# Holding a background decode back at the stage boundaries of a hybrid decoder step, with ScalarE's reads of a bank first and the last tile scaled late

## The chip, the cores and the metric

The kernel runs on one core of one Trainium2 chip. Its time is the device time of one execution in microseconds (us), as the median of several runs; lower is better. TensorE (PE in the profile) multiplies matrices into banks of the accumulation memory, VectorE (DVE), ScalarE (ACT) and GpSimd (POOL) work elementwise, and SyncE (SP) issues most of the transfers (DMAs). Every engine runs its own queue in order and waits on semaphores for the others.

## The reference

One layer of a hybrid decoder step, for two groups that share the weights: a prompt of 1024 rows and 8 sample rows with 8192 past tokens each, in a paged cache.

```python
h = rmsnorm(x) @ w_in                      # q, k, v (8 heads x 64), forget logits, u, z
att = softmax(q k^T / 8 + c_q - c_k, causal) @ v      # c: cumulated log-forget
sgu = u * (tril(w_s) applied to chunks of 128 of rmsnorm(z) + b_s)
x = x + concat(rmsnorm(att), rmsnorm(sgu)) @ w_o
x = x + cross_attention(rmsnorm(x), 256 memory tokens, 4 heads x 256) @ w_co
h = rmsnorm(x) @ w_up                      # 1024 -> 2 x 2816
hc = conv_b + sum_i conv_w[i] * h shifted by 2 - i rows      # causal, depthwise
x = x + (silu(gate(hc)) * val(hc)) @ w_down
y = rmsnorm(x)
```

For the sample rows the attention runs over the cache (`cache_k`, `cache_v`, gathered by a page table), and the convolution over a stored state. All of it is float32. The kernel returns both outputs and the new keys, values, log-forget gates, memory keys and values and convolution states.

## The kernel before

**Products.** Each large product is made of three: both operands are split into a rounded high part and a rest, and `gemm3` (L244, L245, L246) sums high x high, high x rest and rest x high. `split` makes the parts: ScalarE copies the high part (L207, or L210 with a scale), VectorE subtracts for the rest (L208, L211). Weights come through SyncE's queue as 512 KB pieces (`wr`) and are split into `wh` and `wl`. I call these three lines' 5568 matmuls the main matmuls, and count positions on TensorE by them.

**The prompt line.** `prompt()` is a generator. It runs the input projection (stage p1), the attention of both halves of 512 rows (att0, att1), and then for each half: `merge`, an output projection (`out_proj` with `w_o`), the cross stage (mid0, mid1; `norm_T`, queries, scores, and `out_proj` with `w_co`), the gated MLP (`ffn0`, `ffn1`: `norm_T`, then groups of up products with the convolution, and down products), and `final`. Each `yield` gives a cost in units of its work.

`out_proj` works on four tiles of 128 rows, two column halves each. `residual` adds the product to the rows (L905) and takes the sum of squares of each half (L202). For a projection whose rows are normalised next, `prepare(i)` adds both halves' sums on VectorE (L910), takes mean and EPS on VectorE (L195) and the power -1/2 on POOL (L196), and ScalarE scales the tile (L921). The last tile's is queued under `high_priority`.

`norm_T` transposes the first three tiles together on TensorE (L954), splits the eight transposed blocks (L210, L211) and runs the first product on these 384 columns; then it transposes the fourth tile (L968), splits it, and runs the product's other 128 columns.

In the convolution ScalarE reads a bank (L1132), VectorE reads it twice (L1133, L1134), and ScalarE reads its last two columns for the state (L1135); then the bank is free.

**The background.** `sample()` is a second generator with the sample rows' work: 128 steps on the keys (`kstep`: an indirect load of 1 MB into one of four `kv` buffers by POOL, L1246, a product and a reduction on VectorE, L1252 and L1256), softmax, 128 steps on the values (a load, L1305, and four matmuls, L1311), and then the rest: projections, the cross attention over the stored memory (VectorE's L1475 and L1476 on `kv`), 22 up steps (a 1 MB load, L1550, and eight matmuls, L1554; every second one followed by a fold, L1569), 11 down steps (a 1 MB load, L1588, and four matmuls, L1593) and the last sum (L1606). A load goes out when one of the four buffers is free.

The loop that emits both lines adds up the prompt line's units and advances the background by one step for every `PACE` units of the stage:

```python
PACE = {'p1': 7.5, 'att0': 20.0, 'mid0': 8.0, 'ffn0': 9.0, 'att1': 15.0, 'mid1': 7.5, 'ffn1': 2.5, 'rest': 3.3}
...
        acc[0] += t
        while bgs and acc[0] >= PACE[phase[1] or phase[0]]:
            acc[0] -= PACE[phase[1] or phase[0]]
            if next(bgs[0], None) is None:
                bgs.pop()
```

What is emitted goes through a scheduler that simulates the engines and fixes each engine's queue at build time. So the order on an engine follows the emission only loosely: what counts is where the built program puts an instruction.

Of the kernel before, what the change touches and what calls it, by code (L numbers as in the profile page):

```python
# [18 lines left out]
P = 128  # L19
D = 1024  # L20
# [58 lines left out]
def build(nc, tc, ctx, a, phases=None):  # L79
# [81 lines left out]
    nc.vector.memset(mhalf, -0.5)  # L161
    warm = const.tile([P, 1], F32, tag="warm", name="warm")
# [144 lines left out]
    def p1(early):  # L307
# [119 lines left out]
        for tt in range(8):  # L427
            ps, ps2 = BK(), BK()
            mm_chunk(tt, ws, ps[:, 0:260], 0, 260)
            mm_chunk(tt, ws, ps2[:, 0:260], 260, 260)  # L430
            if tt == SD - 1:
                sps = [sample_copy(*sp) for sp in sps]
            if tt == SD:
                sp = sample_sum(*sps[0])
                nc.scalar.activation(us, sp, AF.Gelu_apprx_tanh, scale=rsk)
                sp = sample_sum(*sps[1])
                nc.vector.scalar_tensor_tensor(fs, sp, rsk, bfb[:8], op0=ALU.mult, op1=ALU.add)
            nc.vector.scalar_tensor_tensor(fl[:, tt, :], ps[:, 0:8], rstd[:, tt : tt + 1], bfb, op0=ALU.mult, op1=ALU.add)
            u = T2()
            nc.scalar.activation(u[:, 0:252], ps[:, 8:260], AF.Gelu_apprx_tanh, scale=rstd[:, tt : tt + 1])  # L440
            nc.scalar.activation(u[:, 252:512], ps2[:, 0:260], AF.Gelu_apprx_tanh, scale=rstd[:, tt : tt + 1])
            nc.scalar.dma_start(sgu_d[tt * P : (tt + 1) * P, :], u)
            yield 5.4
# [111 lines left out]
    def gating(hf):  # L555
# [44 lines left out]
        r = rstd_of(ssu, AW, 4, "r4")  # L600
        for pr_ in range(2):
# [50 lines left out]
    def attention(hf, late=None, at=3):  # L652
# [16 lines left out]
        def setup(hp, qn, kn, vn):  # L669
# [4 lines left out]
            for j in range(2):  # L674
# [5 lines left out]
                nc.vector.tensor_tensor(qq[64:128, 0, :], tr[rows, :], qq[0:64, 0, :].bitcast(F32), op=ALU.subtract)  # L680
# [9 lines left out]
                nc.gpsimd.dma_start(kb[j][64:68, :], ck_d[h, :, : nk * P])  # L690
            for kh in range(hf + 1):
# [5 lines left out]
                for j in range(2):  # L697
                    rows = slice(64 * j, 64 * j + 64)
                    nc.scalar.activation(ka[j][0:64, s], tr[rows, :], AF.Copy)
                    if KP & 1 << hf:  # L700
                        nc.gpsimd.tensor_copy(ka[j][64:128, s], ka[j][0:64, s].bitcast(F32))
                    else:
                        nc.scalar.activation(ka[j][64:128, s], tr[rows, :], AF.Copy)
                    nc.vector.tensor_tensor(kb[j][0:64, s], tr[rows, :], ka[j][0:64, s].bitcast(F32), op=ALU.subtract)
# [149 lines left out]
    def close(hf, att):  # L854
# [4 lines left out]
        r = rstd_of(ssa, AW, 4, "r4")  # L859
        for b2 in range(2):  # L860
# [4 lines left out]
            nc.sync.dma_start(an_d[t0 * P : (t0 + 2) * P, :].rearrange("(c p) d -> p c d", p=P), att[b2])  # L865

# [30 lines left out]

    def squares():
        return sm([P, 4, 2], "sqx", 2)
# [13 lines left out]
    def out_proj(w, mh, ml, xt, fetch=None, ys=None):  # L913

        sq = squares()

        def prepare(i):
            r = rows_rstd(sq, i, i + 1)
# [3 lines left out]
            ys.append(y)  # L922

        korder = (4, 5, 6, 7, 0, 1, 2, 3)
        for n in range(2):
# [5 lines left out]
            for i in range(4):  # L931
# [6 lines left out]
                if ys is not None and n == 1 and i > 0:  # L938
                    prepare(i - 1)
                residual(xt, sq, i, n, ps)  # L940
                yield 5.2
        if ys is not None:
            with tc.high_priority():
                prepare(3)
        return sq

    def norm_T(ys, g0, first):
# [3 lines left out]
        for kk in range(8):  # L951
# [8 lines left out]
            if kk % 2:  # L960
                yield 0.8
        first(hs, ls, slice(0, 384))
# [8 lines left out]
        first(hs, ls, slice(384, 512))  # L971
        return hs, ls
# [126 lines left out]
    def ffn(hf, xt, ys, late=None):  # L1099
# [18 lines left out]
        for gi, gn in enumerate(GROUPS):  # L1118
            gh, gl = [], []
            for f in range(f0, f0 + gn):  # L1120
                hc2 = []
                for part in range(2):
# [9 lines left out]
                    nc.scalar.activation(hc, pv, AF.Identity, bias=cb, scale=cw[2])  # L1132
                    nc.vector.scalar_tensor_tensor(hc[:, 1:], pv[:, :511], cw[1], hc[:, 1:], op0=ALU.mult, op1=ALU.add)  # L1133
                    nc.vector.scalar_tensor_tensor(hc[:, 2:], pv[:, :510], cw[0], hc[:, 2:], op0=ALU.mult, op1=ALU.add)  # L1134
                    nc.scalar.activation(hlast[hf][:, ft, :], pv[:, 510:512], AF.Copy)  # L1135
# [504 lines left out]
    def prompt():  # L1640
# [26 lines left out]
        close(0, att)  # L1667
# [3 lines left out]
        else:  # L1671
            att = yield from att1
        ends = []
        for hf in range(2):
# [27 lines left out]
    for t in prompt():  # L1702
# [7 lines left out]
        while bgs and acc[0] >= PACE[phase[1] or phase[0]]:  # L1710
# [96 lines left out]
```

## Time and profile before

| | before |
|---|---|
| median of 3 runs | 1917.92 us (1917.23 to 1918.78) |
| the profiled execution's own time | 1925.17 us |
| its span in the trace | 1923.4 us |
| mean granted TensorE clock | 0.976 |
| busy: PE, DVE, ACT, POOL | 94%, 73%, 40%, 23% |
| moved by DMA | 517.07 MB, mean 269 GB/s |

Times in the trace are counted from the start of its span. A row of the chain of waits gives the waiting engine, tile and line, what released it, and the sum, the number and the longest of these waits. A row in order of time gives start, duration, engine, line, operation, output from inputs, shapes and count, and in brackets how long the engine had been idle before and what released it. Equal instructions that follow each other stand in one row, and a matmul of float32 operands leaves two records. A row of a window gives the stretch, then for PE, PEld (weight loads), DVE, ACT and POOL the busy time and the count, and at the end the granted clock, the share of the DMA engines that was busy and the GB/s.

### The profile page before, as it was taken

The numbers are of one execution on the slowest core, as the hardware profiler recorded it, in microseconds if no ns is written. First come the engines' busy times: TensorE is split into PE (matmuls) and PEld (weight loads), VectorE is DVE, ScalarE is ACT, GpSimd is POOL, SyncE is SP. The second block draws the span as 40 slices with busy tenths as digits, with TensorE's granted clock in tenths as the row PEclk, the third lists the DMA queues.
The fourth block names the chain that finished last, engine by engine and source line by source line (L and its number), as shares of the span: only waits on it lengthen the run. The fifth ranks groups of instructions, "written<-read, shape, count | busy, mean of one in ns | idle before, by whom it ended". The sixth has DMA issues, their size and how long they took to land.

```text
span 1923.4 us, 24228 instructions
## 1 busy us (share of the span) xinstructions
PE 1817.3 (94%) x9255; PEld 1300.1 (68%) x9255; DVE 1407.5 (73%) x1679; ACT 763.6 (40%) x1419; POOL 446.1 (23%) x427
## 2 busy tenths in 40 slices
PE   8999989888898998999999999998989999899998
PEld 5987667555576666777777776765756667667765
DVE  4887567877678768889899899878785548754344
ACT  5332366576532534433334234326234333242232
POOL 1222241222022323222112315131332012101110
PEclk9999999999998998999999999999989999999999
DMA  8876887744587858678777889977698657667972
GB/s 325 290 266 222 296 328 262 249 145 164 183 328 295 310 208 296 254 262 328 271 271 268 321 299 354 357 293 281 248 342 339 221 206 261 223 244 241 321 280 101
DMA packets 156372, 517.07 MB, mean 269 GB/s; under 512 B 20168, under 2 KB 41928, under 8 KB 123488
## 3 DMA queue, kind: packets, MB, share of 16 engines
q0 software_dynamic: 56400, 339.04, 47.4%
q1 hardware_dynamic: 92944, 163.89, 24.4%
q10 hardware_dynamic: 6912, 12.59, 1.7%
q8 instruction: 73, 1.20, 0.2%
q14 instruction: 43, 0.35, 0.1%
HBM read 493.63 MB, written 21.84 MB: 268 GB/s over the span
## 4 chain that ended last, share of the span: by engine, by line
PE 63%; DVE 7%; issue 6%; DMA 3%; ACT 2%; POOL 1%; POOLq 0%; DVEq 0%; ACTq 0%
PE ba L244 11%; PE ba L246 10%; PE ba L245 10%; PE bb L245 5%; PE bb L244 5%; PE bb L246 5%; PE dv L1311 5%; DVE kv L1252 1%; DVE s L1256 1%; PE dv L1554 1%; DVE wl L208 1%; DMA kv<-cache_v,kidx 1%; DMA t<-o_mk 1%; PE bb L763 1%; PE ba L719 1%
## 5 line engine op out<-in xcount | busy, mean ns | idle before, releaser
L207 ACT ACTIVATE wh<-wr 128x1024 fp32r<-128x1024 f32 (+2 forms) x220 | 228.9, 1044 | 410.8 <-PE ba L245 125.1
L208 DVE TENSOR_TENSOR wl<-wr,wh 128x1024 fp32r<-128x1024 f32 (+2 forms) x220 | 261.8, 1202 | 169.0 <-PE ba L246 73.3
L1252 DVE TENSOR_TENSOR kv<-kv,d 128x2048 f32<-128x2048 f32 (+1 forms) x139 | 292.2, 2114 | 34.7 <-DMA kv<-cache_k,kidx 34.7
L1256 DVE TENSOR_REDUCE s<-kv 128x32 f32<-128x2048 f32 (+1 forms) x139 | 291.9, 2107 | 0.7
L1246 POOL DMA_INDIRECT kv<-cache_k,kidx x128 | 166.0, 1297 | 487.1 <-DVE s L1256 242.1
L1305 POOL DMA_INDIRECT kv<-cache_v,kidx x128 | 159.8, 1249 | 490.3 <-PE dv L1311 196.0
L244 PE MATMUL ba<-wh,u 128*128 128x512 f32 (+1 forms) x679 | 261.5, 388 | 7.6 <-ACT u L210 3.9
L245 PE MATMUL ba<-wl,u 128*128 128x512 f32 (+1 forms) x679 | 259.7, 383 | 0.0
L246 PE MATMUL ba<-wh,u 128*128 128x512 f32 (+1 forms) x679 | 256.9, 383 | 0.4 <-DVE u L208 0.4
L244 PE MATMUL ba<-u,wh 128*128 128x512 f32 (+2 forms) x552 | 218.9, 397 | 0.0
L245 PE MATMUL ba<-u,wh 128*128 128x512 f32 (+2 forms) x552 | 216.9, 394 | 0.0
L246 PE MATMUL ba<-u,wl 128*128 128x512 f32 (+2 forms) x552 | 216.6, 393 | 0.0
L244 PEld LDWEIGHTS ba<-wh,u 128*128 128x128 f32 x679 | 129.0, 190 | 43.3 <-issue 9.5
L245 PEld LDWEIGHTS ba<-wl,u 128*128 128x128 f32 x679 | 128.8, 190 | 30.5 <-issue 5.5
L246 PEld LDWEIGHTS ba<-wh,u 128*128 128x128 f32 x679 | 128.4, 189 | 29.7 <-issue 3.4
L244 PEld LDWEIGHTS ba<-u,wh 128*128 128x128 f32 x552 | 105.7, 192 | 42.4 <-issue 14.5
L1311 PE MATMUL dv<-kv,s 128*32 128x512 f32 x1024 | 133.1, 620 | 0.1
L245 PEld LDWEIGHTS ba<-u,wh 128*128 128x128 f32 x552 | 106.2, 192 | 29.3 <-issue 8.4
L246 PEld LDWEIGHTS ba<-u,wl 128*128 128x128 f32 x552 | 105.7, 192 | 28.8 <-issue 6.8
L244 PE MATMUL bb<-wh,u 128*128 128x512 f32 (+1 forms) x313 | 120.7, 386 | 4.1 <-ACT hlast L1135 4.1
L245 PE MATMUL bb<-u,wh 128*128 128x512 f32 (+2 forms) x312 | 123.8, 397 | 0.6 <-DVE u L211 0.6
L244 PE MATMUL bb<-u,wh 128*128 128x512 f32 (+2 forms) x312 | 123.3, 395 | 0.1
(403 smaller groups left out, 2940.2 us busy)
## 6 DMA issues: line engine op xcount, KB each, us to landing
wr<-w_up SPq DMA_DIRECT2D x88, 512.0 KB
kv<-w_up POOLq DMA_DIRECT2D x22, 1024.0 KB, 8.1
wr<-w_down SPq DMA_DIRECT2D x40, 512.0 KB
kv<-w_down POOLq DMA_DIRECT2D x11, 1024.0 KB, 6.4
wr<-w_in SPq DMA_DIRECT2D x16, 512.0 KB
wr<-w_o SPq DMA_DIRECT2D x16, 512.0 KB
wr<-w_cq SPq DMA_DIRECT2D x16, 512.0 KB
wr<-w_co SPq DMA_DIRECT2D x16, 512.0 KB
```

The costliest lines, as they stand in the source:

```text
L207: nc.scalar.activation(h, src, AF.Copy)
L208: nc.vector.tensor_tensor(l, src, h.bitcast(F32), op=ALU.subtract)
L244: mmul(out, sh, mh, start=(i == 0), stop=False)
L245: mmul(out, sh, ml, start=False, stop=False)
L246: mmul(out, sl, mh, start=False, stop=(i == n - 1))
L719: mmul(s, qab[j][:, 0, i * P : (i + 1) * P], ka[j][:, ch * n : ch * n + n], start=True, stop=False)
L763: mmul(po[64 * j : 64 * j + 64, q0:256], vn[:, kt, 64 * j : 64 * j + 64], pt[j][kt // 4][:, kt % 4, q0:256], start=(kt == 0), stop=(kt == ...
L1246: nc.gpsimd.indirect_dma_start(kv, None, a["cache_k"], off(kidx[:, b, ch : ch + 1]))
L1252: nc.vector.tensor_tensor(kvv[:, i : i + m, :], kvv[:, i : i + m, :], qb.unsqueeze(1).broadcast_to((P, m, 512)), op=ALU.mult)
L1256: nc.vector.tensor_reduce(s[:, ch * 4 + i : ch * 4 + i + m, :].rearrange("p k h -> p (k h)"), kvv[:, i : i + m, :].rearrange("p k (h d) -> ...
L1305: nc.gpsimd.indirect_dma_start(kv, None, a["cache_v"], off(kidx[:, b, ch : ch + 1]))
L1311: mmul(dv[32 * j : 32 * j + 32, :], s[:, ch * 4 : ch * 4 + 4, :].rearrange("p k h -> p (k h)"), kvv[:, j, :], start=(ch == 0), stop=(ch == ...
```

## The change

- **Hold.** A flag `held` is set with the last tile of an `out_proj` and cleared at the end of the next `norm_T`. While it is set the loop advances no background step. The loop also takes at most `int(t / PACE) + 1` steps after one unit of the prompt line.
- **The factor.** `prepare` is split. `factor(i)` sums on ScalarE (the first half's sum goes through an Identity with EPS as bias into `part`, the second through another with `part` as bias), and POOL takes the power; VectorE has no part in it. `scaled` multiplies on ScalarE. For the last tile `scaled` is kept as a partial call, which `norm_T` makes after the splits of the first three tiles.
- **ScalarE first.** In the convolution the read of the last two columns moves ahead of VectorE's two reads. In the attention's set-up ScalarE reads both halves of a bank before VectorE subtracts from them. In the input projection the gelu of a bank stands ahead of VectorE's read of it.
- **Small pieces.** `stats` makes its two factors with two powers on POOL instead of one, a copy and a product. `close` (sums of squares and scaling of the attention's output) becomes a generator, whose steps run beside the attention of half 1 and beside `merge` instead of at once. `gating` has one more `yield`.

```diff
@@ stats, input projection
-            r = rstd_of(ssx[:, c], D, 4, "r4")
-            nc.vector.tensor_copy(rstd[:, c], r)
-            nc.vector.tensor_scalar(rstd8[:, c], r, 0.125, None, op0=ALU.mult)
+            for dst, m in ((rstd8, 64.0), (rstd, 1.0)):
+                v = sm([P, 4], "xv", 2)
+                nc.vector.tensor_scalar(v, ssx[:, c], m / D, m * EPS, op0=ALU.mult, op1=ALU.add)
+                nc.gpsimd.tensor_tensor(dst[:, c], v, mhalf[:, :4], op=ALU.pow)
...
@@ attention set-up
-                nc.vector.tensor_tensor(qq[64:128, 0, :], tr[rows, :], qq[0:64, 0, :].bitcast(F32), op=ALU.subtract)
...
+            for j, qq in enumerate(qab):
+                rows = slice(64 * j, 64 * j + 64)
+                nc.vector.tensor_tensor(qq[64:128, 0, :], tr[rows, :], qq[0:64, 0, :].bitcast(F32), op=ALU.subtract)
...
@@ close
         for i in range(4):
             ssq_into(ssa[:, i : i + 1], att[i // 2][:, i % 2, :])
-        r = rstd_of(ssa, AW, 4, "r4")
+        yield
+        r = rstd_of(ssa, AW, 4, "ra")
+        yield
...
+    def beside(main, steps, at):
+        n = 0
+        while True:
+            try:
+                t = next(main)
+            except StopIteration as e:
+                return e.value
+            yield t
+            if n in at:
+                next(steps)
+            n += 1
...
@@ out_proj
-        def prepare(i):
-            r = rows_rstd(sq, i, i + 1)
+        part = sm([P, 4], "part", 2)
+
+        def factor(i):
+            r = sm([P, 1], f"fac{i}", 2)
+            nc.scalar.activation(r, sq[:, i, 1:2], AF.Identity, scale=1.0 / D, bias=part[:, i : i + 1])
+            nc.gpsimd.tensor_tensor(r, r, mhalf[:, 0:1], op=ALU.pow)
+            return r
+
+        def scaled(i, r):
             y = U([P, D])
             for c in (slice(0, 512), slice(512, D)) if i == 3 else (slice(0, D),):
                 nc.scalar.activation(y[:, c], xt[i][:, c], AF.Copy, scale=r)
-            ys.append(y)
+            return y
...
                 if ys is not None and n == 1 and i > 0:
-                    prepare(i - 1)
+                    ys.append(scaled(i - 1, factor(i - 1)))
                 residual(xt, sq, i, n, ps)
+                if ys is not None and n == 0:
+                    nc.scalar.activation(part[:, i : i + 1], sq[:, i, 0:1], AF.Identity, scale=1.0 / D, bias=epsb)
+
+                held[0] = n == 1 and i == 3
                 yield 5.2
         if ys is not None:
             with tc.high_priority():
-                prepare(3)
+                ys.append(partial(scaled, 3, factor(3)))
@@ norm_T
+        if callable(ys[3]):
+            ys[3] = ys[3]()
         first(hs, ls, slice(0, 384))
         yield 4
...
         first(hs, ls, slice(384, 512))
+        held[0] = False
@@ ffn, convolution
                     nc.scalar.activation(hc, pv, AF.Identity, bias=cb, scale=cw[2])
+                    nc.scalar.activation(hlast[hf][:, ft, :], pv[:, 510:512], AF.Copy)
                     nc.vector.scalar_tensor_tensor(hc[:, 1:], pv[:, :511], cw[1], hc[:, 1:], op0=ALU.mult, op1=ALU.add)
                     nc.vector.scalar_tensor_tensor(hc[:, 2:], pv[:, :510], cw[0], hc[:, 2:], op0=ALU.mult, op1=ALU.add)
-                    nc.scalar.activation(hlast[hf][:, ft, :], pv[:, 510:512], AF.Copy)
@@ prompt
-        close(0, att)
+        ending = close(0, att)
+        next(ending)
...
-            att = yield from att1
+            att = yield from beside(att1, ending, (0, 2))
+        ending = close(1, att)
+        next(ending)
...
-            mh, ml = yield from merge(*got.pop())
+            mh, ml = yield from beside(merge(*got.pop()), ending, (3, 7)) if hf == 0 else merge(*got.pop())
...
-            if hf == 0:
-                close(1, att)
@@ the loop
         acc[0] += t
-        while bgs and acc[0] >= PACE[phase[1] or phase[0]]:
+        most = int(t / PACE[phase[1] or phase[0]]) + 1
+        while bgs and not held[0] and most and acc[0] >= PACE[phase[1] or phase[0]]:
+            most -= 1
             acc[0] -= PACE[phase[1] or phase[0]]
```

In the built programs the matmuls are the same in number. VectorE loses 17 instructions, ScalarE gains 16 and POOL 2.

More of the change, by code (lines that the diff above doesn't have):

```diff
@@ L161, in build @@
     nc.vector.memset(mhalf, -0.5)
+    epsb = const.tile([P, 1], F32, tag="epsb", name="epsb")
+    nc.vector.memset(epsb, EPS)
     warm = const.tile([P, 1], F32, tag="warm", name="warm")
@@ L437, in p1 @@
                 nc.vector.scalar_tensor_tensor(fs, sp, rsk, bfb[:8], op0=ALU.mult, op1=ALU.add)
-            nc.vector.scalar_tensor_tensor(fl[:, tt, :], ps[:, 0:8], rstd[:, tt : tt + 1], bfb, op0=ALU.mult, op1=ALU.add)
             u = T2()
             nc.scalar.activation(u[:, 0:252], ps[:, 8:260], AF.Gelu_apprx_tanh, scale=rstd[:, tt : tt + 1])
+            nc.vector.scalar_tensor_tensor(fl[:, tt, :], ps[:, 0:8], rstd[:, tt : tt + 1], bfb, op0=ALU.mult, op1=ALU.add)
             nc.scalar.activation(u[:, 252:512], ps2[:, 0:260], AF.Gelu_apprx_tanh, scale=rstd[:, tt : tt + 1])
@@ L600, in gating @@
         r = rstd_of(ssu, AW, 4, "r4")
+        yield 1
         for pr_ in range(2):
@@ L703, in setup @@
                         nc.scalar.activation(ka[j][64:128, s], tr[rows, :], AF.Copy)
+                for j in range(2):
+                    rows = slice(64 * j, 64 * j + 64)
                     nc.vector.tensor_tensor(kb[j][0:64, s], tr[rows, :], ka[j][0:64, s].bitcast(F32), op=ALU.subtract)
@@ L865, in close @@
             nc.sync.dma_start(an_d[t0 * P : (t0 + 2) * P, :].rearrange("(c p) d -> p c d", p=P), att[b2])
+        yield
+    def beside(main, steps, at):
[9 more added lines that the diff above has]
+            n += 1
     def merge_in(hf):
@@ L896, in merge @@
         return mh, ml
+    held = [False]
     def squares():
```

## The prediction

> **What bounds the kernel now.** I read the page first, then the chain of waits of TensorE, then the order of time at the places where TensorE waits longest, and last the windows with rates.
>
> ```profile
> PE 1817.3 (94%) x9255; PEld 1300.1 (68%) x9255; DVE 1407.5 (73%) x1679; ACT 763.6 (40%) x1419; POOL 446.1 (23%) x427
> PE ba L954 <- DVE u L211: 14.8, 3, 8.6
> PE ba L968 <- DVE u L211: 5.5, 5, 2.5
> PE ba L578 <- DVE u L570: 4.6, 2, 4.1
> PE bb L244 <- ACT hlast L1135: 4.1, 1, 4.1
> PE ba L244 <- ACT hlast L1135: 3.4, 1, 3.4
> PE ba L719 <- DVE u L680: 3.1, 2, 2.7
> ```
>
> TensorE is busy for 1817.3 of 1923.4 us, so 106 us is all that can be won without taking matmuls away. The other rows (who waits, on what; us in total, times, longest) say where a part of it lies: at the starts of a `norm_T` (L954, L968), where transposed tiles wait for VectorE's half of a split (L211), and in the convolution (L1135). The change aims at both. It does not change TensorE's work: both built programs hold the same matmuls. So the time moves by the idle time that goes or comes, and by stretches at half clock behind it.
>
> **The ffn of half 0: its boundary.** In order of time (start, us, instruction, idle before):
>
> ```profile
> 746.26 2.28 DVE L1252 TENSOR_TENSOR kv<-kv,d 128x2048 f32<-128x2048 f32 x1
> 746.39 1.15 ACT L921 ACTIVATE u<-u,rn2r 128x1024 f32<-128x1024 f32 x1 [0.43 <-POOL rn2r L196]
> 749.66 2.28 DVE L1256 TENSOR_REDUCE s<-kv 128x32 f32<-128x2048 f32 x1
> 751.86 0.14 DVE L195 TENSOR_SCALAR rn3r<-rq 128x1 f32<-128x1 f32 x1
> 753.78 1.33 ACT L921 ACTIVATE u<-u,rn3r 128x512 f32<-128x512 f32 x2 [2.59 <-POOL rn3r L196]
> 756.36 0.61 DVE L211 SCALAR_TENSOR_TENSOR u<-ba,gp,u 128x384 fp32r<-128x384 f32 x1
> 757.03 0.90 PE L954 MATMUL ba<-cp,u 128*128 128x128 f32 x3 [8.56 <-DVE u L211]
> 757.00:762.20 5.20, 5.17 (x18) 5.16 (x19) 5.20 (x8) 2.10 (x4) 0.00 (x0) 0.50 0.97 314
> ```
>
> The last tile's factor (L195) stands on VectorE behind a decode step's L1256; ScalarE, in order, waits for it in L921, and the splits of the three finished tiles stand behind L921. TensorE loses 8.56 us, then runs 5.2 us at a granted clock of 0.50 (the last row, second number from the end but two), which costs another 2.6. In the changed order no decode operation stands here, the factor is made by ScalarE (about the 0.17 us of the small reads shown below) and POOL, and L921 of the last tile stands behind all first splits. ScalarE is then the limit: L921 of the third tile still ends near 748, then come a split or two, a weight split and two sums of squares. That lets the first L211 start near 751 instead of 756.36 and the last L968 split come 4 to 5 us earlier. With the clock between nothing and 2.6 back: 4 to 9; I take 6.5, a us of displaced decode matmuls taken off.
>
> **The ffn of half 1: its boundary.**
>
> ```profile
> 1400.79 1.92 PE L1311 MATMUL dv<-kv,s 128*32 128x512 f32 x16
> 1402.79 2.28 DVE L1256 TENSOR_REDUCE s<-kv 128x32 f32<-128x2048 f32 x1
> 1408.74 0.62 DVE L211 SCALAR_TENSOR_TENSOR u<-ba,gp,u 128x384 fp32r<-128x384 f32 x1 [2.68 <-ACT u L210]
> 1409.51 0.88 PE L954 MATMUL ba<-cp,u 128*128 128x128 f32 x3 [5.58 <-DVE u L211]
> 1422.26 2.28 DVE L1252 TENSOR_TENSOR kv<-kv,d 128x2048 f32<-128x2048 f32 x1
> 1424.86 0.47 PE L968 MATMUL ba<-cp,u 128*128 128x128 f32 x1 [2.50 <-DVE u L211]
> 1424.40:1431.20 6.80, 6.34 (x22) 3.55 (x23) 5.36 (x7) 1.10 (x3) 1.96 (x3) 0.50 0.95 364
> 1445.55 0.39 PE L245 MATMUL ba<-u,wh 128*128 128x512 f32 x1
> ```
>
> Here one decode step stays in the changed order ahead of the splits (L1252, L1256); its L1256 ends near 1404.8, and eight L211 of 0.6 us follow at once, where the first came at 1408.74. Behind them no decode step is left, against six operations of 2.28 us among the late splits of before. Eight transposes with splits of the last tile (one after another a transpose, a ScalarE and a VectorE half of 0.3 to 0.6 us each, by my estimate 1.3 to 1.5 with the handovers), from about 1410, end near 1422; with the twelve L1311 that stay in this stretch the matmul of 1445.55 comes near 1431. That is 14 us earlier, but 20 L1311 and their like leave the stretch and must be done elsewhere on TensorE. The row at 1400.79 prices them: eight instructions (16 records) 1.92 us, so 20 cost 4.8. Net 9, from 5 (the last tile's chain slower) to 11.
>
> **The convolution of half 1.**
>
> ```profile
> 1635.52 2.28 DVE L1476 TENSOR_REDUCE sS<-kv 128x8 f32<-128x2048 f32 x1
> 1637.71 0.74 DVE L1134 SCALAR_TENSOR_TENSOR t<-bb,gp,t 128x510 f32<-128x510 f32 x1
> 1638.48 0.17 ACT L1135 ACTIVATE hlast<-bb 128x2 f32<-128x2 f32 x1 [4.89 <-DVE t L1134]
> 1638.71 0.49 PE L244 MATMUL bb<-wh,u 128*128 128x512 f32 x1 [4.11 <-ACT hlast L1135]
> 1649.95 0.80 PE L244 MATMUL ba<-wh,u 128*128 128x512 f32 x1 [3.39 <-ACT hlast L1135]
> 1649.95:1653.30 3.35, 3.35 (x8) 2.67 (x9) 3.35 (x4) 0.64 (x2) 0.44 (x1) 0.53 0.53 218
> ```
>
> The wait names L1135, but the bank was held by L1134, behind the sample rows' L1475 and L1476. Putting the read ahead saves 0.2 us a time and no more; TensorE would then wait for L1134. What removes the two stalls is that L1475 and L1476 are scheduled later, into the down projection, where VectorE has little to do. 4.11 + 3.39, and a stretch of about 3.4 us at a clock of 0.53 behind each (1.6 lost in each): 0 to 11, I take 8.
>
> **The two cross stages, the attention, the rest.** In cross of half 0, L1252 and L1256 still stand among the splits and ahead of L570, which ended the 4.1 us wait of L578; eight of the 16 L1311 that filled TensorE move behind. What one loses the other gives: 0, from 4 slower to 3 faster. Cross of half 1 keeps its three pairs: +0.5 (-2 to 3). In the attention set-up two ScalarE reads now stand before two subtractions; the nearest row is the 3.1 us of L719 behind L680, taken as the bound both ways: 0. The two `pow` in `stats`, `fl` behind a gelu, and `close` in steps are covered by engines at 40% and 23%; their cover gone, they cost a few operations of 0.14 to 0.6 us, under 2 us together. VectorE loses 17 operations, ScalarE gains 16. Sum of gains: 6.5 + 9 + 8 + 0 + 0.5 = 24 (10 to 34).
>
> **What is paid: the tail.** Holding steps back and limiting the catch-up moves the decode later. In the built orders, counted in main matmuls (5568 in all), the last decode L1311 moves from 4246 to 4421, the first up step (L1554) from 5121 to 5389. Of the 22 up steps and 11 down steps (one 1 MB load each, four `kv` buffers), 14 stand before number 5523; eight up steps, all eleven down steps and L1606 stand back to back at 5523, and only 45 main matmuls behind them.
>
> ```profile
> kv<-w_down POOLq DMA_DIRECT2D x11, 1024.0 KB, 6.4
> 1764.54 1.07 PE L1554 MATMUL dv<-kv,xsT 128*32 128x256 f32 x16
> 1765.54 1.06 PE L1569 MATMUL ms<-cp,d 128*128 128x8 f32 x8
> 1866.84 1.06 PE L1593 MATMUL dv<-kv,d 128*32 128x512 f32 x4
> 1867.72 1.03 PE L1593 MATMUL ms<-kv,d 128*32 128x512 f32 x4
> 1898.80 1.88 PE L1606 MATMUL ba<-d,cp 128*8 128x512 f32 x4
> 1905.11 0.40 PE L246 MATMUL ba<-wh,u 128*128 128x512 f32 x1
> 1398.00:1430.00 32.00, 23.45 (x126) 14.97 (x124) 27.66 (x29) 11.70 (x23) 12.84 (x10) 0.81 0.89 344
> 1409.50:1414.20 4.70, 4.59 (x18) 2.51 (x19) 4.70 (x7) 2.50 (x6) 0.82 (x1) 0.50 1.01 424
> 1860.00:1870.00 10.00, 10.00 (x45) 6.82 (x44) 6.34 (x10) 4.48 (x8) 1.80 (x3) 1.00 0.99 396
> ```
>
> Number 5523 ran at 1905.11. The work moved behind it takes 8 x 1.0 (up steps) + 4 x 1.0 (their folds, L1569) + about 16.5 (eleven down steps, at most 1.84 each, some packed closer) + 1.9 (L1606) = 30 us, so the changed kernel comes there at 1905.3 - 30.4 = 1874.9, less the gains. Two of the next loads have landed, two are under way; 17 MB of 1.049 million bytes, 17.8 in all, have still to flow, and a load is asked for only when a step has freed a buffer. A step costs 1.0 to 1.84 us, a load 1.049 MB / 396 GB/s = 2.65 (the last number of the windows is GB/s), so TensorE waits for loads. I take 396, the window filled by just such loads: 45 us. The last step, the copies and L1606 add 5: 50 us. At 424 it is 47, at 344, 57. Then the same 18.1 us as before from 1905.3 to 1923.4. The end: 1874.9 + 50 + 18.1 = 1943.0 less 24 = 1919.0, 4.4 under the span of 1923.4. The median of the runs, 1917.92, lies 5.5 under that span; so I forecast 1913.5.
>
> The Trainium skill, "DMA: Bandwidth & Descriptors", section "Where 436 GB/s comes from", says that for HBM to SBUF the HBM side, about 358 GB/s, binds. By it the stream would take 49.8 instead of 45 us and the gain would be nil; the rows of 396 and 424 speak against it as a limit, and no row shows a stream of 45 us.
>
> **The rivals.** (1) Slower: the tail binds harder than I think. The mechanism is the stream of 17 loads behind four buffers, its place number 5523 to L1606. It speaks for it that the long window, 32 us, has 344 GB/s, and against it that this window had other work to wait for. At 344 the stream costs 7 more, at half clock the 45 last matmuls 3.4 more: 30 us paid; with gains at 15 the time is 1917.9 + 15 = 1933. It decides as soon as the tail costs more than the boundaries give, at 24. The page's rule on HBM lies on this side. (2) Much faster: all boundaries give their upper end, 34, and the stream runs at 424 for 16.6 paid: 1900.5. For it speaks that the idle time is there in the rows; against it, that ScalarE's queue replaces VectorE's as the limit. (3) The stalls only change place: held steps come back in the convolution, where VectorE is already nearly full and TensorE would wait on it at L1134; the gains shrink to nothing and the tail stays: 1917.9 + 20 = 1938. Against it stands a row of the convolution of half 0, in which VectorE is busy for 346.54 of 380 us and TensorE never idle:
>
> ```profile
> 800.00:1180.00 380.00, 380.00 (x1770) 279.39 (x1769) 346.54 (x328) 135.14 (x208) 95.39 (x74) 1.00 0.79 292
> ```
>
> That the order is not what was built is excluded by the trace of before, which runs in the built order.
>
> **How the numbers follow.** A measurement of this kernel can tell 0.2%, 3.8 us. The forecast has 0.50, its own range 1905 to 1921 (tail 17 to 23, gains 20 to 28 and some of each the other way); of it 0.32 lies beyond 3.8 us faster, 0.12 within, 0.06 beyond on the slow side. Rival 1 has 0.30 (0.26 slower, 0.04 same), rival 2 0.12, rival 3 0.08. Faster 0.44, same 0.16, slower 0.40. The range 1900 to 1935 leaves out half of rival 3 and the far ends of the others.
>
> **What would show it.** In the changed profile: no wait over 5 us in L954; none on L1135 or L1134 near the sample rows' L1476; main matmul 5523 near 1851; then TensorE waiting on `kv` loads 17 times for 1 to 2 us, 18 to 20 us in all, at about 396 GB/s. I am wrong if the stretch from 5523 to L1606 lasts under 45 or over 57 us, if a boundary waits as long as before, or if waits over 3 us turn up where before had none.

## The result, and the profile after: slower

| | before | changed |
|---|---|---|
| median, us | 1917.92 (1915.81 to 1926.38, 10 runs) | 1926.51 (1921.58 to 1931.42, 10 runs) |
| ratio of the runs | | 1.0038, 95% interval 1.0027 to 1.0050 |
| profiled execution: own time, span, us | 1925.17, 1923.4 | 1927.71, 1926.0 |
| mean granted clock | 0.976 | 0.971 |

The change costs 0.38%, some 7 us (these two medians differ by 8.6), where 4.4 us less were forecast. The time lies inside the range, on the wrong side. In the changed kernel the lines are numbered anew: L213 is the split's L211, L992 and L1008 are `norm_T`'s L954 and L968, L955 is L921, L1176 is L1134, L1595 and L1610 are the up steps' L1554 and L1569, L1634 is the down steps' L1593, L1647 is L1606. The page of the changed kernel (busy times; then the granted clock in 40 slices), and the rows of its chain of waits that answer to those of before:

```profile
PE 1821.5 (95%) x9255; PEld 1305.7 (68%) x9255; DVE 1403.7 (73%) x1662; ACT 761.3 (40%) x1435; POOL 470.1 (24%) x429
PEclk9999999889999999999999999999999999999978
PE dv L1634 <- DMA kv<-w_down: 7.4, 4, 3.2
PE ba L992 <- DVE u L213: 4.4, 3, 2.2
PE ba L1008 <- DVE u L213: 1.3, 3, 0.5
PE dv L1595 <- DMA kv<-w_up: 1.3, 1, 1.3
```

The boundaries opened: L992 waits 4.4 us for the splits instead of 14.8, L1008 1.3 instead of 5.5, and no row of L1135 is left. What is new are the waits of the sample steps (L1634, L1595), and a low clock in the last two slices. In order of time, the boundary of the first MLP:

```profile
746.54 1.15 ACT L955 ACTIVATE u<-u,fac 128x1024 f32<-128x1024 f32 x1 [0.83 <-POOL fac L949]
747.88 0.46 PE L992 MATMUL bb<-cp,u 128*128 128x128 f32 x2 [2.12 <-DVE u L932]
749.20 0.62 DVE L213 SCALAR_TENSOR_TENSOR u<-ba,gp,u 128x384 fp32r<-128x384 f32 x1 [0.24 <-ACT u L212]
752.55 0.44 PE L246 MATMUL ba<-u,wh 128*128 128x384 f32 x1 [1.14 <-DVE u L213]
754.66 1.38 ACT L955 ACTIVATE u<-u,fac 128x512 f32<-128x512 f32 x2
```

The first L213 starts at 749.20 (756.36 before), and the last tile is scaled at 754.66, behind splits and no longer in front of them. And the pile at main matmul 5523:

```profile
1848.81 1.07 PE L1595 MATMUL dv<-kv,xsT 128*32 128x256 f32 x16
1855.97 1.07 PE L1595 MATMUL dv<-kv,xsT 128*32 128x256 f32 x16 [1.33 <-DMA kv<-w_up]
1857.76 1.87 PE L1610 MATMUL ms<-cp,d 128*128 128x8 f32 x8 [0.72 <-ACT d L1605]
1859.56 3.66 PE L1595 MATMUL dv<-kv,xsT 128*32 128x256 f32 x32
1863.99 1.88 PE L1610 MATMUL ms<-cp,d 128*128 128x8 f32 x8 [0.78 <-ACT d L1605]
1870.22 1.88 PE L1610 MATMUL ms<-cp,d 128*128 128x8 f32 x8 [0.78 <-ACT d L1605]
1874.69 1.96 PE L1634 MATMUL dv<-kv,d 128*32 128x512 f32 x8 [2.60 <-issue]
1884.16 1.33 PE L1634 MATMUL dv<-kv,d 128*32 128x512 f32 x4 [3.23 <-DMA kv<-w_down]
1906.24 0.50 PE L246 MATMUL ba<-wh,u 128*128 128x512 f32 x1
```

From 1848.8 to 1906.2 TensorE runs sample steps alone: 57.4 us for work that takes 30.4 when it is spread among main matmuls. Its windows (the first row is the whole pile), and POOL's issues of the loads:

```profile
1848.80:1906.20 57.40, 42.33 (x260) 16.69 (x260) 2.78 (x6) 4.29 (x8) 11.04 (x16) 0.76 0.83 313
1855.00:1871.50 16.50, 13.26 (x102) 7.84 (x103) 0.00 (x0) 1.79 (x3) 3.57 (x5) 0.58 1.02 397
1871.50:1881.00 9.50, 6.83 (x35) 2.22 (x35) 1.42 (x4) 0.81 (x2) 2.14 (x3) 0.66 0.72 222
1881.00:1891.00 10.00, 6.84 (x24) 1.38 (x24) 0.00 (x0) 0.00 (x0) 1.43 (x2) 0.83 1.01 408
```
```profile
1868.07 0.71 POOL L1629 DMA_DIRECT2D kv<-w_down  x1 [3.81 <-PE dv L1595]
1869.78 0.71 POOL L1629 DMA_DIRECT2D kv<-w_down  x1 [0.99 <-PE dv L1595]
1878.54 1.42 POOL L1629 DMA_DIRECT2D kv<-w_down  x2 [8.05 <-PE ms L1634]
```

So 57.4 is 15.1 us of idle time and 42.33 of work, 11.9 more than the 30.4, at a mean granted clock of 0.76.

In two long windows the loads flow at 397 and 408 GB/s (at 337 in the first 6 us, 1848.7 to 1855.0). But POOL issues none between 1869.78 and 1878.54: all four buffers are taken by weights of the down projection, which cannot be used before the up projection's last sum has gone through ScalarE and VectorE (the 2.60 us at 1874.69), and the first down steps then run at a granted clock of 0.66. So the rate falls to 222 GB/s for 9.5 us.

Where the time went is best read from the same main matmuls in several traces (us from the start of each span; the third column is a second execution of the kernel before, the last one the run with a changed pace, told below):

| main matmul | before | before again | changed | changed, PACE 8.0 |
|---|---|---|---|---|
| 1344, cross of half 0 begins | 573.5 | 576.3 | 573.0 | 571.6 |
| 1753, first of ffn 0 | 758.2 | 761.4 | 752.6 | 752.3 |
| 3660, in cross of half 1 | 1274.5 | 1276.4 | 1267.8 | 1271.0 |
| 3960, last ahead of ffn 1 | 1398.3 | 1395.4 | 1393.8 | 1404.9 |
| 4060, in ffn 1 | 1445.6 | 1441.7 | 1427.7 | 1431.4 |
| 4421, decode done in all | 1556.4 | 1552.6 | 1535.9 | 1543.2 |
| 5523, ahead of the pile | 1905.1 | 1901.5 | 1848.4 | 1887.7 |
| 5524, behind it | 1905.3 | 1901.8 | 1906.2 | 1887.9 |
| 5568, the last | 1915.5 | 1912.0 | 1916.5 | 1898.1 |

The changed kernel comes to 5523 56.7 us earlier than the first trace of before; 30.4 of these are work that it has not done yet, 26.3 are won (22.7 against the second trace). Between 5523 and 5524 it gives all of it back.

### The profile page after: what moved, and what is told of

It reads as the page before. It is cut to its first block, busy times and chain, and to the rows that moved or that the text cites. A ratio compares the mean times of both kernels' runs of the same rounds, so it can differ in the third digit from the quotient of the medians.

```text
span 1926.0 us, 24250 instructions
## 1 busy us (share of the span) xinstructions
PE 1821.5 (95%) x9255; PEld 1305.7 (68%) x9255; DVE 1403.7 (73%) x1662; ACT 761.3 (40%) x1435; POOL 470.1 (24%) x429
## 4 chain that ended last, share of the span: by engine, by line
PE 64%; DVE 6%; issue 6%; ACT 3%; POOL 1%; DMA 1%; POOLq 0%; DVEq 0%; ACTq 0%
PE ba L246 11%; PE ba L247 11%; PE ba L248 11%; PE bb L246 5%; PE dv L1352 5%; PE bb L247 5%; PE bb L248 5%; DVE kv L1293 1%; DVE s L1297 1%; PE ba L1078 1%; PE bb L772 1%; PE ba L728 1%; PE bb L756 1%; PE ba L1104 1%; DMA kv<-w_down 1%
## 5 line engine op out<-in xcount | busy, mean ns | idle before, releaser
L1287 POOL DMA_INDIRECT kv<-cache_k,kidx x128 | 172.1, 1345 | 493.6 <-DVE s L1297 191.0
L1346 POOL DMA_INDIRECT kv<-cache_v,kidx x128 | 171.0, 1336 | 487.8 <-DVE s L1297 216.1
L248 PE MATMUL bb<-u,wl 128*128 128x512 f32 (+2 forms) x312 | 122.4, 392 | 0.0
```

Of the source, the lines that this page charges most:

```text
L248: mmul(out, sl, mh, start=False, stop=(i == n - 1))
L1287: nc.gpsimd.indirect_dma_start(kv, None, a["cache_k"], off(kidx[:, b, ch : ch + 1]))
L1346: nc.gpsimd.indirect_dma_start(kv, None, a["cache_v"], off(kidx[:, b, ch : ch + 1]))
```

## The experiments

The theory (A): the boundaries gained what they promised, and the pile of sample steps that the later decode causes costs more than that. The rivals: (B) held steps come back as waits where they are put; (C) the hold opens the boundaries, the other edits do nothing; and that reading order alone helps, as the waits on L1135 seem to say. The limit on the catch-up and the small pieces were not run by themselves.

| run | what | median, us | ratio to before, 95% interval |
|---|---|---|---|
| changed | | 1926.5 | 1.0038 (1.0027 to 1.0050) |
| e1 | changed, PACE of ffn0 8.0 | 1908.6 | 0.9944 (0.9922 to 0.9966) |
| e2 | changed, no hold and no limit | 1915.9 | 0.9982 (0.9970 to 0.9995) |
| e3 | before, hold alone | 1939.6 | 1.0108 (1.0083 to 1.0134) |
| e4 | changed, half of the sample up matmuls left out | 1919.1, one execution | |
| e5 | before, a second trace | 1921.6, one execution | |
| e6 | before, read orders alone | 1919.3 | 0.9990 (0.9973 to 1.0008) |
| e7 | before, late scaling and factor alone | 1911.9 | 0.9962 (0.9946 to 0.9978) |
| e8 | changed, PACE of ffn0 8.5 | 1930.8 | 1.0059 (1.0038 to 1.0080) |
| e9 | before, PACE of rest 2.6 | 1939.3 | 1.0105 (1.0090 to 1.0120) |
| e10 | e2 with PACE of ffn0 8.0 | 1911.6 | 0.9961 (0.9946 to 0.9977) |
| e11 | e7 with PACE of ffn0 8.0 | 1914.8 | 0.9980 (0.9965 to 0.9994) |
| e12 | changed, PACE 8.0, 7.0, 6.5 in ffn0, mid0, mid1 | 1908.1 | 0.9949 (0.9936 to 0.9963) |

### e1: the pile taken away by the pace

```diff
-PACE = {..., 'ffn0': 9.0, ...}
+PACE = {..., 'ffn0': 8.0, ...}
```

> The changed kernel with one number altered: PACE of ffn0 8.0 instead of 9.0, so that more decode steps are emitted in the first MLP. In the built order the last decode L1311 stands at main matmul 4223 (changed kernel 4421, before 4246) and no pile of sample steps is left: the up steps stand from 5122 to 5342, the down steps to 5478. Theory A (the boundaries gave some 20 us or more, the pile at 5523 took them): the boundaries stay as good, the 27 us of the pile go, so 1926.5 - 27 = about 1900 (1894 to 1908). Rival B (the held steps come back as waits wherever they are put): 1915 to 1925, with waits in the convolutions in place of the pile.

1908.6 us, 0.9944. The pile is gone, and with it the 0.9% between this run and the changed kernel: 18 us, from one number. It missed the expected 1900 and just the edge of 1908: in this order the sample rows' reductions lie in the second convolution again, and the wait that the changed kernel had lost returns, on VectorE this time (chain of waits of e1):

```profile
PE bb L246 <- DVE t L1178: 6.2, 1, 6.2
```

L1178 is the step behind L1176, the last read of the bank by VectorE. The cross of half 1 takes longer, too: from main matmul 3660 to 3960 it is 133.9 us, 126.0 in the changed kernel. The gain at the convolution came from where the reductions stood, as the prediction had it.

### e2 and e10: no hold

```diff
-                held[0] = n == 1 and i == 3
+                held[0] = False
...
-        most = int(t / PACE[phase[1] or phase[0]]) + 1
-        while bgs and not held[0] and most and acc[0] >= PACE[phase[1] or phase[0]]:
-            most -= 1
+        while bgs and not held[0] and acc[0] >= PACE[phase[1] or phase[0]]:
```

> The changed kernel without the hold and without the limit on the catch-up; late scaling, the factor on ScalarE, the read orders and the small pieces stay. The built order has no pile (up steps 5122 to 5342, down steps to 5482, last L1311 at 4265). Theory A: no tail is paid, and the late scaling alone opens the first MLP's boundary; 1908 to 1916. Rival C (nothing but the hold helps): as before, 1916 to 1920. Rival B: 1905 or less cannot be reached; if it is, the hold was of no use at all.

0.9982: taking the hold and the limit out of the changed kernel makes it 0.56% faster. At 1915.9 us that lies between A's range (to 1916) and C's (from 1916), and the interval reaches into both, so the time does not decide between them; e7 does. The trace shows why no more, waits in the cross stages (L1096, 2.6 us in the same row of the changed kernel) and again at L992:

```profile
PE ba L1096 <- ACT u L1089: 12.7, 3, 7.4
PE ba L992 <- DVE u L213: 8.2, 3, 5.0
```

e10 is e2 with PACE of ffn0 at 8.0 (`'ffn0': 9.0` to `'ffn0': 8.0`), to be set beside e1:

> The changed kernel without the hold and the limit, and with PACE of ffn0 at 8.0, beside the run with the hold and 8.0 (0.9944 of before). No pile in either built order (here up steps 5083 to 5303, down steps to 5452). Theory D (late scaling gives nearly all of the gain, the hold hardly adds): 0.993 to 0.997. Rival C (the hold is what opens the boundaries): 0.998 or more.

0.9961 without the hold, 0.9944 with it, neither with a pile. That is in D's range and outside C's, so most of the gain comes without the hold. That it is nearly all late scaling's is not shown: by itself it has 0.9980 at this pace (e11) and 0.9962 at 9.0 (e7), and the intervals overlap. The 0.17% between e10 and e1 is less than the intervals' width, so what the hold itself is worth once nothing piles up is not settled; it is between nothing and some 8 us.

### e3: the hold alone

```diff
+    held = [False]
...
                 residual(xt, sq, i, n, ps)
+                held[0] = n == 1 and i == 3
                 yield 5.2
...
         first(hs, ls, slice(384, 512))
+        held[0] = False
         return hs, ls
...
-        while bgs and acc[0] >= PACE[phase[1] or phase[0]]:
+        while bgs and not held[0] and acc[0] >= PACE[phase[1] or phase[0]]:
```

> The kernel before with the hold alone (the flag from an output projection's last tile to the end of norm_T), none of the other edits. In the built order 27 sample steps stand back to back at main matmul 5478, against 19 at 5523. Theory A: some 25 loads have to flow in the pile; at 308 GB/s, as in the changed kernel's pile, 85 us less 42 us of TensorE work moved there is 43 paid, and the hold without late scaling gives 10 to 15: 1918 + 30 = about 1948 (1935 to 1955). Rival (the pile is harmless): 1905 to 1915.

1939.6 us, 1.0108, inside A's range. The pile of 27 steps took 77.0 us between main matmuls 5478 and 5479. The hold makes the pile: it is enough by itself, and e2, without it, has none.

### e9: the pile alone

```diff
-PACE = {..., 'rest': 3.3}
+PACE = {..., 'rest': 2.6}
```

> The kernel before with one number altered: PACE of the rest 2.6 instead of 3.3. Nothing is held and no boundary changes; in the built order the last 15 sample steps (4 up, 11 down) and L1606 stand back to back at main matmul 5282 instead of being spread to 5503. Theory A (a pile costs by itself, whatever made it): 13 loads at the 3.4 us each of the changed kernel's pile are 44 us, less 24 us of TensorE work moved there: 20 paid, 1.008 to 1.013 of before. Rival (the changed kernel's tail cost came from the hold or from being last): 0.998 to 1.003.

1.0105, 20.1 us on 1918.6: what A said, with no hold and no boundary touched. Its pile of 15 steps, from 1815.7 to 1864.8, is the same picture as the changed kernel's: half clock in the up steps, then a pause of the loads and a wait for them (order of time, then windows):

```profile
1825.08 3.64 PE L1554 MATMUL dv<-kv,xsT 128*32 128x256 f32 x32
1833.97 1.96 PE L1593 MATMUL dv<-kv,d 128*32 128x512 f32 x8 [2.59 <-issue]
1843.51 1.93 PE L1593 MATMUL dv<-kv,d 128*32 128x512 f32 x4 [2.58 <-DMA kv<-w_down]
```
```profile
1823.00:1834.00 11.00, 7.35 (x50) 5.01 (x52) 1.42 (x4) 1.64 (x4) 2.03 (x3) 0.50 0.98 378
1834.00:1848.00 14.00, 11.42 (x48) 2.76 (x48) 0.00 (x0) 0.00 (x0) 3.56 (x5) 0.67 0.79 298
```

### e4: what sets the pile's length

```diff
-                for k in range(8):
+                for k in range(4):
...
-                        start=(k < 4),
-                        stop=(k >= 4),
+                        start=True,
+                        stop=True,
```

> The changed kernel with half of the sample up projection's matmuls left out (k below 4 only), loads unchanged; the output of the sample rows is not the reference's. Read in the trace: the stretch from main matmul 5523 to L1647, 57.8 us in the changed kernel, and in it the four groups of two up steps and a fold, 6.24 us each at a granted clock of 0.5. If TensorE at half clock sets the up steps (theory A1), a group falls to the 5.3 us that its 2 MB need and the stretch to 50 to 54 us. If the loads set them (A2), groups and stretch stay as they are, 56 to 58 us.

One execution: the stretch took 54.9 us (1842.7 to 1897.6, starts of main matmuls 5523 and 5524, against 57.9 for the same two in the changed kernel), the groups of two up steps and a fold 5.2 us instead of 6.2. So at half clock TensorE does set the pace of the up steps, as A1 says; but the stretch hardly shortens, 3 us where 4 to 8 were expected, because TensorE now waits 3.19 us for a load of up weights at 1850.88 (1.33 at 1855.97 in the changed kernel) and the four buffers are full of down weights again:

```profile
1857.86 1.88 PE L1610 MATMUL ms<-cp,d 128*128 128x8 f32 x8 [0.78 <-ACT d L1605]
1862.98 1.88 PE L1610 MATMUL ms<-cp,d 128*128 128x8 f32 x8 [0.78 <-ACT d L1605]
1867.46 1.96 PE L1634 MATMUL dv<-kv,d 128*32 128x512 f32 x8 [2.60 <-issue]
1877.90 1.52 PE L1634 MATMUL dv<-kv,d 128*32 128x512 f32 x4 [4.01 <-DMA kv<-w_down]
```

Whether a fifth buffer would shorten that pause was not tried.

### e5, e6, e7: the parts by themselves

> The kernel before, unchanged, for a second trace of it: the first one's execution took 1925.2 us where the median is 1918. Expected 1916 to 1920, and the stretch in which the first trace lost its 7 us seen by the times of the same main matmuls. If the first trace's boundaries were typical, number 5523 comes at 1898 and the waits at L954 and L1135 are the same.

1921.6 us in that execution. The waits of the boundary and of the convolution are there again (8.6 us at L954; 4.1 and 2.3 at L1135, 4.1 and 3.4 in the first trace). But the cross stage of half 1 is passed from main matmul 3660 to 3800 in 77.9 us, against 82.7 in the first trace. The first trace lost 5 us there, 3.0 of them in one wait for a load (L1021 at 1325.34). And the changed kernel needs longer still for the stage. Its windows from 3660 to 3960, in the first trace, the second and the changed kernel:

```profile
1274.50:1398.30 123.80, 118.98 (x548) 82.62 (x548) 95.99 (x92) 52.16 (x106) 34.65 (x30) 0.99 0.76 286
1276.40:1395.40 119.00, 117.18 (x549) 81.87 (x548) 95.74 (x92) 52.01 (x106) 34.71 (x30) 1.00 0.79 298
1267.80:1393.80 126.00, 120.63 (x565) 81.64 (x564) 99.68 (x89) 53.43 (x113) 44.49 (x31) 1.00 0.77 294
```

The traces of e6 and e9, which have before's order in this stage, take 118.9 us, and that of e4, which has the changed kernel's, 126.0 again. So 119 is the usual time, and the changed kernel pays 7 us here: 1.9 for 16 more records of decode matmuls, the rest mostly in idle time (5.4 us against 1.8). Set against the first trace alone, this loss hardly shows.

Number 5523 came at 1901.5 and not at 1898, since this execution lost some 3 us earlier, in the attention.

```diff
-                nc.vector.tensor_tensor(qq[64:128, 0, :], ...)      # set-up: moved behind both copies
...
                     nc.scalar.activation(hc, pv, AF.Identity, bias=cb, scale=cw[2])
+                    nc.scalar.activation(hlast[hf][:, ft, :], pv[:, 510:512], AF.Copy)
...
-                    nc.scalar.activation(hlast[hf][:, ft, :], pv[:, 510:512], AF.Copy)
```

> The kernel before with the order of reads alone (ScalarE first in the convolution, in the attention's set-up and in the input projection). Theory A: nothing, 0.999 to 1.001 of before, since each bank is held by VectorE's reads; the waits of 4.1 and 3.4 us in the second convolution stay, now put down to VectorE's L1134 instead of ScalarE's L1135. Rival: the reads gain what the waits name, 3 to 8 us (0.996 to 0.9985).

0.9990 (0.9973 to 1.0008): nothing that can be told from none, though the interval alone does not exclude the rival's smaller gains. The trace speaks against them: from main matmul 4060 to 5121 TensorE is idle for 7.8 us, 7.5 and 6.5 in the two traces of before. The convolution's wait stays and only changes its name, L1141 being VectorE's step behind the last read of the bank (order of time of e6):

```profile
1627.60 2.36 DVE L1479 TENSOR_TENSOR kv<-kv,d 128x1024 f32<-128x1024 f32 x2
1629.87 0.75 DVE L1139 SCALAR_TENSOR_TENSOR t<-bb,gp,t 128x510 f32<-128x510 f32 x1
1630.77 0.47 PE L244 MATMUL bb<-wh,u 128*128 128x512 f32 x1 [2.29 <-DVE t L1141]
```

e7 takes `factor`, `scaled`, `part` and the late call in `norm_T` from the change, and nothing else:

```diff
-                    prepare(i - 1)
+                    ys.append(scaled(i - 1, factor(i - 1)))
...
-                prepare(3)
+                ys.append(partial(scaled, 3, factor(3)))
...
+        if callable(ys[3]):
+            ys[3] = ys[3]()
         first(hs, ls, slice(0, 384))
```

> The kernel before with the factor on ScalarE and the last tile scaled late, no hold, no limit, no other edit. In the built order no pile (up steps 5145 to 5365, down steps to 5507, last L1311 at 4279). Theory A: the first MLP's boundary opens, its 8.56 us wait falls below 5 and the second one's somewhat: 0.996 to 0.999 of before. Rival C (only the hold opens the boundaries, decode operations of 2.28 us still stand among the splits): 0.999 to 1.002.

0.9962, so 7 us faster, with decode operations still among the splits: A, and against C. In its chain of waits the longest of the boundary falls from 8.6 to 4.4 us, and the first product behind the second boundary waits 4.9:

```profile
PE ba L966 <- DVE u L213: 7.3, 3, 4.4
PE ba L246 <- DVE u L213: 4.9, 1, 4.9
```

The hold by itself opens the boundaries, too. From main matmul 3960 to 4060 the kernel before takes 47.2 us, e3 33.1, e7 38.2, the changed kernel 33.9. Taking off the decode matmuls that left the stretch (48, 16 and 40 records at 0.12 us, by the row at 1400.79 of the kernel before), they gain 8.3, 7.1 and 8.5. From 1752 to 1753 the times are 15.1, 10.8, 9.9 and 8.3. So at the second boundary either edit alone gives nearly what both give; these are single executions.

e11 is e7 with the same edit of PACE, `'ffn0': 9.0` to `'ffn0': 8.0`:

> The kernel before with the late scaling and the factor on ScalarE alone (0.9962 of before at PACE 9.0), here with PACE of ffn0 at 8.0, so that the decode ends earlier (last L1311 at 4183, up steps 5076 to 5296, down steps to 5448, no pile). Theory A: 0.994 to 0.998, no more than before, since the tail was not what bound that kernel. Rival: an earlier decode is worth something by itself: under 0.993.

0.9980, at the edge of A's range and far from the rival's: the earlier decode is worth nothing here by itself; the intervals of e7 and e11 overlap.

### e8 and e12: other paces

```diff
-PACE = {..., 'ffn0': 9.0, ...}
+PACE = {..., 'ffn0': 8.5, ...}      # e8
...
-PACE = {..., 'mid0': 8.0, 'ffn0': 9.0, ..., 'mid1': 7.5, ...}
+PACE = {..., 'mid0': 7.0, 'ffn0': 8.0, ..., 'mid1': 6.5, ...}      # e12
```

> The changed kernel with PACE of ffn0 at 8.5 (9.0 in the changed kernel, 8.0 in the run before this one, which took 0.9944 of the kernel before and had a wait of 6.2 us at VectorE's L1178 behind the sample rows' reductions in the second convolution). In the built order half of those reductions move out of the convolution (main matmuls 4716 to 4812 instead of 4592 to 4748), and a pile of only five steps stands at 5463. Theory A: the wait in the convolution mostly goes, 4 to 7 us; the pile costs 0 to 5: 0.990 to 0.995 of before. Rival (a small pile costs as a large one does): over 0.998.

1.0059, a miss of theory A's forecast, and on the rival's side. From main matmul 5121, where both have nearly the same work behind them, to the last one it loses 6.5 us against the first trace of before (2.1 ahead, then 4.4 behind): somewhat more than the 0 to 5 given to its small pile, and far less than a large one costs. The rest is lost earlier. The reductions that were to leave the convolution now stand close together at its end and at the start of the down projection, eight of them from 4712 to 4824 by their starts in the trace, and hold up a weight split and a residual there:

```profile
PE ba L246 <- DVE u L1207: 6.8, 1, 6.8
PE ba L247 <- DVE wl L210: 3.9, 1, 3.9
```

From main matmul 4768 to 4844 this run takes 33.6 us, with VectorE busy for 33.41 of them; the first trace of before takes 18.3. That is rival B, in one place. In the changed kernel the same eight stand between 4781 and 4986, and no wait shows.

> The changed kernel, hold and all, with PACE 8.0 in ffn0, 7.0 in mid0 and 6.5 in mid1 (9.0, 8.0 and 7.5): decode earlier still (last L1311 at 4161, up steps 5076 to 5296, down steps to 5424, no pile). Theory A: as the run with ffn0 at 8.0 alone or a little better, 0.990 to 0.996. Rival B (held and hurried steps fill VectorE and TensorE waits for it in the cross stages): over 0.997.

0.9949, like e1 and in A's range, although the cross of half 1 takes 139.7 us from 3660 to 3960, some of it decode work moved there. e1 and e12 are faster than both kernels: 1908.6 and 1908.1 us, against 1918 and 1926.5.

## Why the prediction was wrong

Two terms of the sum failed: the tail, which cost 57.4 us and not 50, and the 5.5 us between span and median, which the changed kernel does not have. Point by point, against the trace:

- **The gains** (24 forecast to 5523, from 10 to 34): 26.3, the arrival at 1848.4 where 1851 was forecast; 22.7 against the second trace. Right in sum, but in part by luck, since the terms missed both ways. The first MLP's boundary gave 6.8 us (main matmul 1753 goes from 1.1 later at 1752 to 5.7 earlier), 1.9 of it 16 displaced records of decode matmuls, so 4.9 where 6.5 were written; the second one's 13.3 us to main matmul 4060, of which 4.8 are displaced L1311, so 8.5 for 9. In the convolution the two waits are gone, 7.5 us and the clock behind them; from 4060 to 5523 it is 13.3 (38.9 earlier, less the 30.4 not yet done, plus 4.8 of decode work moved in) for 8. The cross of half 0 is worth little, as forecast. The cross of half 1 was forecast at +0.5 (-2 to 3): against the first trace, which had lost 5 us there, it is 2.2 slower, against the usual 119 us 7. The reason given for the convolution, that the read order would change nothing and the place of L1475 and L1476 everything, is what e6 and e1 show.
- **The tail** (50 us forecast, 47 to 57): 57.4. This is the step that failed first, and the error is 7.4 us. The rate was right: 397 and 408 GB/s in the windows where loads flowed, for 396. What was wrong was "TensorE waits for loads" all the way. In the up steps TensorE at half clock sets the pace, as e4 shows; its work in the pile took 42.3 us, not 30.4. And the loads wait, too: with four buffers full of down weights they stop from 1869.78 to 1878.54 until the up projection's sum is through and slow down steps have freed a buffer, so that the mean rate of the pile is 313 GB/s. Seventeen waits for loads, 18 to 20 us, were to show it; there are five, 8.7 us (rows L1634 and L1595 of the chain of waits), in 15.1 us of idle time.
- **Behind the pile**: 19.8 us from 5524 to the end instead of 18.1, 1.7 more.
- **From the span to the median**: this step failed by 6 us. The profiled execution of before was slow by 7 us against its median, 5 of them in the cross of half 1 (e5), and I took its 5.5 us between span and median for the changed kernel, too. Of that one the median lies 0.5 above the span. The difference of two spans, +2.6, said less than the difference of the medians, +8.6, for the same reason.

1913.5 - 2.4 + 7.4 + 1.7 + 6 = 1926.2, against 1926.5. Two of the signs of being wrong came: the tail was over 57 us, and waits over 3 us turned up where before had none (3.2 at L1634; 5.5 at L1096 in the cross of half 0, 2.5 before).

**The rivals.** Rival 1 came true in its sign, its place (5523 to L1606) and nearly its price (30 forecast, 57.4 + 19.8 - 30.4 - 18.1 = 28.7 measured). Its mechanism did so in part: the stream of loads behind four buffers did bind harder, but by a pause and by TensorE at half clock in the pile, where 344 GB/s and half clock in the last 45 matmuls were named; those matmuls, 1906.2 to 1916.5, ran at full clock (and half clock for all of them would have cost 10 us, not the 3.4 written). The limit of about 358 GB/s that the Trainium skill states ("DMA: Bandwidth & Descriptors", section "Where 436 GB/s comes from") does not hold here: the windows of the pile have 397 and 408. Rival 2 had neither its gains (34, measured 26.3) nor its tail (16.6 paid). Rival 3 did not happen in the changed kernel, whose convolutions show no wait, but it did in e8, and e1 shows one wait of it.

The weighing failed with the sum: the gain side was off by 2.4 us and the cost side by 9, and the difference of the two, 4.4, was smaller than the error of the cost. With 24 against 20 the sign was open, and that the time lies inside the range says little for the sum.

## What to carry to other kernels

A background stream that is held back at the boundaries must be given its time back elsewhere: look in the built order where its last steps went before judging what the hold gains, because a few steps with nothing to run beside can cost as much as all the boundaries give (here 27 us for 19 steps, 20 for 15, against 26). Price such a pile by a run of steps that stand alone, not by their price among other work: its buffers fill with what cannot be used yet, and its matmuls run slower. Set a profiled execution against its median before its span is compared with another's; a second trace of the same kernel showed here which stretch had been slow by chance. And when a wait names one reader of a bank, look which reader comes last on a busy queue before reordering them.

## What the runs showed of the hardware

In the up steps of the piles TensorE was granted half its clock without being idle for long. In the changed kernel the up steps' matmuls (32 output rows each, 16 records in 1.07 us at 1848.81) take 3.66 us for 32 records from 1859.56, and no idle time longer than 1.33 us stands in the 9 us ahead of it; from 1862.0 to 1871.5 TensorE was busy for 7.95 of 9.5 us and the granted clock was 0.50:

```profile
1862.00:1871.50 9.50, 7.95 (x58) 4.65 (x51) 0.00 (x0) 1.19 (x2) 2.68 (x4) 0.50 1.01 384
```

e4 and e9 show the same 0.50 in theirs, e4 behind a wait of 3.19 us; in e3 TensorE is busy for 13.50 of the 15.00 us from 1845.0 to 1860.0, at 0.50. The Trainium skill, "TensorE: Matmul & The Clock Gate", section "Part 1", has the half rate set in after at least one idle window of about 3.4 us and lifted by a window of sustained work. The waits of 8.56 and 5.58 us at the boundaries of the kernel before, each with a row of 0.50 behind it, agree with that; the one of 2.50 us at 1424.86, with 0.50 from 1424.4 to 1431.2, does not by its length, and the pile does not by its busy times. What held the clock down there no run shows.
